# Weight-half splits at the change of block: deferred past the first token block's transposes and put on VectorE

## The chip, the cores and the metric

The kernel runs on one core of one Trainium2 chip. The metric is the device time of one execution in microseconds (us); lower is better. The median of three runs of the kernel before is 1123.03 us (1116.99 to 1123.46).

## The reference

The input is x, 256 tokens by 1024 in float32. It goes through one hybrid layer (attention and an mLSTM side by side, output projection, MLP with a squared ReLU), then through two layers of a second kind, and a last norm. All matrix products that matter here have this shape, with everything else left out:

```python
x = x + rms_norm(mixed @ w_out, g_mix_post)            # "out1"; then the MLP
u = jnp.square(jax.nn.relu(rms_norm(x, g_mlp_pre) @ w_up))
x = x + rms_norm(u @ w_down, g_mlp_post)               # "down"; then layer 0 of the second kind
...
mixed = (g_attn * y_attn + g_conv * y_conv) @ w_out[l]
x = x + (1.0 + gate1) * mixed                          # "out2"; then the feed-forward part
h2 = rms_norm_2(x, norm2_g[l]) * (1.0 + scale2) + shift2
f_gate, f_up = jnp.split(h2 @ w_ffn_in[l], 2, axis=-1)
x = x + (1.0 + gate2) * ((jax.nn.silu(f_gate) * f_up) @ w_ffn_out[l])   # "fo"; then the next layer
```

## The kernel before, in words

**Products.** Each float32 product is made of three matmuls in a rounded float32 type (`mm3`, L281): high by high, high by low, low by high. So every operand is split into a high and a low part. For the weights this is `split` (L193): ScalarE (ACT) casts a loaded half `raw` to `whi` (L199), then GpSimd (POOL, L203) or VectorE (DVE, L205) subtracts and writes `wlo`. Which of the two does it is set by an accumulator: `rot["n"]` grows by `rot["pool"]` (0.75 as a rule) at each split, and POOL takes it when 1 is reached, so three in four go to POOL.

**Weight halves.** A half is 128 x 1024 numbers, 512 KB. A planner list (`plan`) holds them in the order of use, with steps for `ada_w` between them. `do_step` (L208) splits the next half and issues the DMA of the half 8 places on (8 `raw` buffers). `pump` (L221) does steps while `made` is under the smaller of `done + 9 - slack` (9 buffers of `whi` and `wlo`) and `rot["cap"]`. Every product that has used up a half calls `done()`, which calls `tick` and so `pump`. All engines work their instructions in program order.

**Change of block.** The 256 tokens are two token blocks, t = 0 and t = 1. Five times a projection ends in `r_tail` (L387), with the last 5 halves ("out1", "out2") or 6 halves ("down", "fo") of its weight, and is followed by a block whose input needs all of it: out1, down, out2 of layer 0, fo of layer 0, out2 of layer 1. A sixth call, at the end of the kernel, has nothing behind it. `r_tail` does all products of t = 0 first, and behind them the first part of `fin(0)`: `post_norm` (L511; out1 and down) or `post_gate` (L525; out2 and fo), that is the residual, its norm, and the scaled row `xn` (L474 on DVE, L475 on ACT). Then come the products of t = 1, half by half, i = 0, 1, and so on. Ahead of i = `CHAIN` (3), `drain_q(chain)` issues `pre_trans(0)` (L486): 8 transposes on TensorE (L494), gains (L500 DVE, L502 ACT), and the split into `hT` (L552 ACT, L553 DVE). Behind the last product follow `fin(1)`'s residual, norm and `xn`.

The next block starts with `a2_block` (L309). It first makes sure that `hold` halves are split (6 behind out1, 8 behind down and fo, 7 behind out2), then does all `hold` halves for t = 0, with `pre_trans(1)` (the call `before(1)`) issued ahead of the last of them, and then t = 1.

**What sets the splits there.** At its start `r_tail` sets `slack` to 0 and pumps, which leaves 4 halves of the next block split (5-half tails) or 3 (6-half tails). Then `rot["cap"] = state["taken"] + cap` with `cap` 6: the `done()` calls of i = 0, 1 (and 2) split 2 (or 3) more, and these stand in the queues of ACT, POOL and DVE ahead of `pre_trans(0)`. The seventh and eighth half are split in `a2_block`, behind `fin(1)`'s `xn`.

Of the kernel before, what the change touches and what calls it, by code (L numbers as in the profile page):

```python
# [21 lines left out]
NL = 2  # L22
FF1 = 4096
FF2 = 2816
# [3 lines left out]
HB, RB, XB = 9, 8, 4  # L28
SLACK = 2
HOLD0, HOLDZ, HOLDF = 8, 8, 7  # L30
CAP = 6
POOL = 0.75
QKV_TAPS, QKV_POOL = 6, 1.0
GATE_TAPS, GATE_POOL = 4, 1.0
# [3 lines left out]
PRE1, PRE2 = 3, 2  # L38
UPC, GAC = (3, 1), (3, 2)
TAIL = 5  # L40
ST = (1, 1, 4, 1)
EARLY, CHAIN, TWO = 1, 3, 0
GATES = 3
LN = (1, 2, 2)
SIG = (1, 2)
# [10 lines left out]
def tile_hybrid_then_diff(ctx: ExitStack, tc: tile.TileContext, I, out: bass.AP):  # L56
# [9 lines left out]
    def acc_tile():  # L66
        return pp.tile([128, 512], FT, name="bank", bufs=8)
# [6 lines left out]
    def st_tile():  # L74
        return sb.tile([128, 8], FT, name="st", bufs=12)
# [88 lines left out]
    at = {}  # L164
# [8 lines left out]

    raws = {}
    halves = {}
    rot = dict(n=0.0, pool=POOL, cap=1 << 30, slack=SLACK, busy=False)
    state = dict(dma=0, step=0, made=0, taken=0, done=0)
    labels = []

# [28 lines left out]
    def do_step():  # L208
        j, h = divmod(state["step"], 2)
        tag, v, kind = plan[j]  # L210
        r = raws.pop((j, h))
        if kind == "a":
            ada_step(tag, r, h)
        else:
            halves[state["made"]] = split(r, (r.shape[1], r.shape[2]))
            labels.append(tag)
            state["made"] += 1
        state["step"] += 1
        issue_dma()

    def pump(most=99):  # L221
        while state["step"] < 2 * len(plan) and most > 0:
            most -= 1
            if plan[state["step"] // 2][2] != "a" and (
                    state["made"] >= min(state["done"] + HB - rot["slack"], rot["cap"])):
                break
            do_step()

    def take(tag):
        i = state["taken"]  # L230
        assert i < state["made"] and labels[i] == tag, (i, state, tag, labels[i:i + 2])
        state["taken"] = i + 1
        return halves.pop(i)
# [75 lines left out]
    def a2_block(seq, xT, before, evac, hold):  # L309
        rot["slack"] = 0  # L310
        rot["cap"] = state["taken"] + hold
        while state["made"] < state["taken"] + hold:
            pump(1)
        rot["slack"] = SLACK
        ws = [take(tag) for tag, _, _, _ in seq[:hold]]

        def half(out, t, b, k0, kn, w):
            for kk in range(kn):
                k = k0 + kk
                mm_tok(out[b][:, 0:1024 // kn], xT, k, t, w, kk, slice(0, 1024 // kn), k == 0, k == 7)  # L320

        before(0)
        outs = []
        for t in range(2):
            if t == 1:
                rot["cap"] = 1 << 30
                if hold == len(seq):
                    evac(0, outs[0])
            outs.append([acc_tile(), acc_tile()])
            for q in range(hold):  # L330
                half(outs[t], t, *seq[q][1:], ws[q])
                if t == 0 and q == hold - 1 - EARLY:
# [12 lines left out]
        rot["busy"] = False
# [38 lines left out]
                mm_tok(acc[t][n], xT, k, t, w, 0, slice(n * 512, n * 512 + 512), start, stop)  # L384
        done()

    def r_tail(tag, srcs, acc, fin, cap, need=None, last=False):  # L387
        rot["slack"] = 0
        pump()
        ws = [take(tag) for _ in srcs]  # L390
        rot["cap"] = state["taken"] + cap
        def mm(t, n, i):
            mm_tok(acc[t][n], srcs[i][0], srcs[i][1], t, ws[i], 0, slice(n * 512, n * 512 + 512),
                   False, i == len(ws) - 1)

        g = fin(0)
        for n in range(2):
            for i in range(len(ws)):
                if need and n == 0:
                    step_gen(fills2)  # L400
                    need(srcs[i][1])
                mm(0, n, i)
            next(g, None)
        chain.append(g)
        rot["busy"] = True
        g = fin(1)
        ahead = range(len(ws) if last else TWO)
        for i in ahead:
            mm(1, 0, i)
        if last:  # L410
            next(g, None)
        for i in range(len(ws)):
            if i == CHAIN:
                drain_q(chain)
            for n in range(1 if i in ahead else 0, 2):
                mm(1, n, i)
            if i == len(ws) - 1:
                if not last:
                    next(g, None)
# [114 lines left out]
    def fin(post, t, acc, grow, gc, bc):  # L534
        st = st_tile()
        made = []

        def xn_of():
            if not made:
                made.append(xn_tile())  # L540
            return made[0]

        yield from post(t, acc, grow, xn_of, st)
        scale_x(t, made[0], st)
        yield
        yield from pre_trans(t, made[0], hT, gc, bc)
# [154 lines left out]
    made = set()  # L701
# [55 lines left out]
    def mod(l, vec, j):  # L757
        assert (l, vec) in made
        return modc[:, l, vec, j:j + 1]
# [54 lines left out]
    def hid_tile():  # L814
        return ab_tile((128, 2, 2, 256), FR)

    def ffn(ng, pre, prefix, up, down_tag, fin, mid=None, last=False):
        hid = {}
        prefix(hid)
        for g in range(pre, LAG):  # L820
            hid[g] = up(g)
        acc = [[acc_tile() for _ in range(2)] for _ in range(2)]
        for g in range(LAG, ng):
            if mid and g == ng - 3:
                mid()
            hid[g] = up(g)
            if g == LAG:
                assert FDEL < 3
                drain_q(fills)
            h = hid.pop(g - LAG)  # L830
            for kk in range(2):
                r_half(down_tag, h, kk, acc, g == LAG and kk == 0, False)
        srcs = [(hid[g], kk) for g in range(ng - LAG, ng) for kk in range(2)]
        r_tail(down_tag, srcs, acc, lambda t: fin(t, acc[t]), CAP, last=last)

    def hid_from_tok(h, full, t):
        ps = ps_tile().rearrange("p (c t) -> p c t", c=4)
# [54 lines left out]
    def before(t):  # L892
        if t == 1:
            run(pre_trans(1, xn[1], hT, lambda j: col0[:, j:j + 1], None))

    def evac(t, acc):
        for a in range(2):
            A.activation(qk[a][:, t, :], acc[a], AF.Copy)

        def gen():  # L900
            for a in range(2):
                rope(qk[a], t, 0)
                yield
# [167 lines left out]
    hT = new_T()  # L1071
    mlp_c = (lambda j: gcol("g_mlp_pre", j), None)
    r_tail("out1", [(mixT, k) for k in range(8 - TAIL, 8)], acc,
           lambda t: fin(post_norm, t, acc[t], gmix, *mlp_c), CAP, need)
    gmlp = row_tile(I["g_mlp_post"])

    def prefix1(hid):
# [33 lines left out]
    def to_layer(l, fin):  # L1111
        gc = lambda j: mod(l, 1, j)
        bc = lambda j: mod(l, 0, j)
        return lambda t, acc: fin(t, acc, gc, bc)

    def end_mlp(t, acc, gc, bc):
# [2 lines left out]
            hT = new_T()  # L1119
        yield from fin(post_norm, t, acc, gmlp, gc, bc)  # L1120

    ffn(FF1 // 256, PRE1, prefix1, up1, "down", to_layer(0, end_mlp))


    for l in range(NL):
# [178 lines left out]
        g1 = gate_tile(l, 2)  # L1304
# [9 lines left out]
        acc = [[acc_tile() for _ in range(2)] for _ in range(2)]  # L1314
        for k in range(8 - TAIL):
# [1 line left out]
        hT = new_T()  # L1317

        r_tail("out2", [(mixT, k) for k in range(8 - TAIL, 8)], acc,
               lambda t: fin(post_gate, t, acc[t], g1, lambda j: mod(l, 4, j), lambda j: mod(l, 3, j)), CAP)  # L1320
        gfin = row_tile(I["final_g_2"], name="vt") if l == NL - 1 else None
        g2 = []

# [40 lines left out]
        def end_all(t, acc):  # L1364
# [6 lines left out]
                nc.sync.dma_start(out[0, t * 128:(t + 1) * 128, n * 512:(n + 1) * 512], u)  # L1371
            yield

        ffn(FF2 // 256, PRE2, prefix2, up2, "fo", end_all if l == NL - 1 else to_layer(l + 1, end_layer),
            lambda: g2.append(gate_tile(l, 5)), l == NL - 1)


# [25 lines left out]
```

## Time and profile before

| what | value |
|---|---|
| median of 3 runs | 1123.03 us (1116.99, 1123.03, 1123.46) |
| profiled execution, its own time | 1118.56 us |
| its span, first to last instruction | 1116.8 us |
| mean granted TensorE clock | 0.979 of full |
| TensorE (PE) busy | 1052.6 us |
| VectorE (DVE), ScalarE (ACT), GpSimd (POOL) busy | 683.3, 559.8, 709.0 us |
| read from memory | 229.63 MB, 207 GB/s over the span |

A span is shorter than the execution's own time by 1.8 us of work around it. A row of a timeline gives the start and duration in us, the engine, the source line, the operation with its tiles, how many were merged into the row, and in square brackets how long the engine had been idle before it and on whom it had waited. Merged rows overlap a little, since operations of one engine are pipelined; a matmul's duration is longer than the distance to the next.

### The profile page before, as it was taken

How to read it: one execution, taken by the hardware profiler on the slowest of the kernel's cores; microseconds unless marked ns; L12 is line 12 of the kernel's file. 1: busy time of each engine (PE TensorE's matmuls, PEld its weight loads, DVE VectorE, ACT ScalarE, POOL GpSimd, SP SyncE). 2: the span in 40 equal slices, each digit the busy share in tenths (PEclk: the TensorE clock that was granted, in tenths of full speed). 3: DMA queues.
4: the chain of work that ended last, by engine and by line, in shares of the span. 5: the costliest groups of instructions: out<-in, count | busy, mean ns of one | idle time of the engine just before them, and what ended most of it. 6: DMA issues, size and time to landing. Idle time of an engine off the chain costs nothing.

```text
span 1116.8 us, 17204 instructions
## 1 busy us (share of the span) xinstructions
PE 1052.6 (94%) x6435; PEld 927.4 (83%) x6435; DVE 683.3 (61%) x1161; ACT 559.8 (50%) x931; POOL 709.0 (63%) x419
## 2 busy tenths in 40 slices
PE   5969989999999899989999998989999899999997
PEld 4756778998897778988798998878889888999995
DVE  2694535999964387835569688645875455642323
ACT  5535556434455546674633333446466555443441
POOL 5753455665686597665566655757958467567671
PEclk9988999999999999999999999999999899999998
DMA  9562244999996375454599989836535366775631
GB/s 317 138 205 94 76 156 146 320 337 311 343 314 202 95 207 171 151 170 152 150 310 314 333 317 340 310 131 191 176 125 165 121 197 203 239 246 188 197 108 38
DMA packets 170191, 231.82 MB, mean 208 GB/s; under 512 B 10983, under 2 KB 110525, under 8 KB 170107
## 3 DMA queue, kind: packets, MB, share of 16 engines
q1 hardware_dynamic: 169979, 230.71, 63.1%
q8 instruction: 50, 0.82, 0.3%
q14 instruction: 34, 0.28, 0.1%
q0 software_dynamic: 128, 0.02, 0.0%
HBM read 229.63 MB, written 1.06 MB: 207 GB/s over the span
## 4 chain that ended last, share of the span: by engine, by line
PE 53%; DVE 15%; POOL 9%; issue 8%; ACT 7%; DMA 6%; SPq 1%; POOLq 0%; DVEq 0%; ACTq 0%
PE bank L282 16%; PE bank L283 16%; PE bank L284 16%; POOL wlo L203 8%; DVE bank L713 3%; ACT whi L199 3%; DMA raw<-in_w_ffn_in_dram 3%; DVE wlo L205 2%; DMA raw<-in_w_down_dram 2%; SPq L426 1%; DVE modc L738 1%; ACT xn L469 1%; PE bank L792 1%; PE bank L791 1%; DMA raw<-in_w_ffn_out_dram 1%
## 5 line engine op out<-in xcount | busy, mean ns | idle before, releaser
L203 POOL TENSOR_TENSOR wlo<-raw,whi 128x1024 fp32r<-128x1024 f32 x262 | 653.6, 2518 | 308.2 <-ACT whi L199 271.5
L199 ACT ACTIVATE whi<-raw 128x1024 fp32r<-128x1024 f32 x332 | 337.2, 1053 | 78.6 <-DMA raw<-in_w_ffn_in_dram 28.4
L282 PE MATMUL bank<-T,whi 128*128 128x256 f32 x1072 | 309.4, 289 | 6.0 <-ACT sc L1347 2.8
L284 PE MATMUL bank<-T,wlo 128*128 128x256 f32 x1072 | 304.6, 284 | 0.0
L283 PE MATMUL bank<-T,whi 128*128 128x256 f32 x1072 | 304.5, 284 | 0.0
L282 PEld LDWEIGHTS bank<-T,whi 128*128 128x128 f32 x1072 | 206.4, 193 | 13.8 <-issue 5.9
L283 PEld LDWEIGHTS bank<-T,whi 128*128 128x128 f32 x1072 | 206.5, 193 | 1.1
L284 PEld LDWEIGHTS bank<-T,wlo 128*128 128x128 f32 x1072 | 206.5, 193 | 0.0
L205 DVE TENSOR_TENSOR wlo<-raw,whi 128x1024 fp32r<-128x1024 f32 x70 | 126.3, 1805 | 91.3 <-ACT whi L199 91.0
L283 PE MATMUL bank<-wlo,T 128*128 128x512 f32 (+1 forms) x432 | 170.3, 394 | 11.4 <-POOL wlo L203 11.4
L282 PE MATMUL bank<-whi,T 128*128 128x512 f32 (+1 forms) x432 | 173.6, 402 | 3.0 <-ACT T L552 1.5
L284 PE MATMUL bank<-whi,T 128*128 128x512 f32 (+1 forms) x432 | 169.4, 392 | 0.0
L713 DVE SCALAR_TENSOR_TENSOR bank<-raw,cact,bank 128x512 f32<-128x512 f32 x168 | 126.8, 755 | 7.1 <-DMA raw<-in_ada_w_dram 1.8
L282 PE MATMUL bank<-whi,AB 128*128 128x512 f32 x304 | 120.7, 397 | 0.0
L284 PE MATMUL bank<-whi,AB 128*128 128x512 f32 x304 | 120.0, 395 | 0.0
L283 PE MATMUL bank<-wlo,AB 128*128 128x512 f32 x304 | 119.9, 394 | 0.0
L283 PEld LDWEIGHTS bank<-wlo,T 128*128 128x128 f32 x432 | 82.9, 192 | 29.7 <-POOL wlo L203 14.2
L1155 DVE SCALAR_TENSOR_TENSOR bank<-cu,cw,bank 128x256 f32<-128x256 f32 x232 | 104.4, 486 | 4.1
L282 PEld LDWEIGHTS bank<-whi,T 128*128 128x128 f32 x432 | 82.8, 192 | 23.2 <-ACT T L552 2.9
L284 PEld LDWEIGHTS bank<-whi,T 128*128 128x128 f32 x432 | 82.7, 191 | 17.5 <-DVE T L553 0.5
L552 ACT ACTIVATE AB<-bank 128x512 fp32r<-128x512 f32 (+1 forms) x49 | 26.0, 538 | 108.3 <-DVE bank L1351 63.7
L284 PEld LDWEIGHTS bank<-whi,AB 128*128 128x128 f32 x304 | 57.2, 188 | 13.4
(264 smaller groups left out, 1164.1 us busy)
## 6 DMA issues: line engine op xcount, KB each, us to landing
raw<-in_w_in_dram SPq DMA_DIRECT2D x96, 512.0 KB, 5.1
raw<-in_ada_w_dram SPq DMA_DIRECT2D x96, 512.0 KB, 7.4
raw<-in_w_ffn_in_dram SPq DMA_DIRECT2D x88, 512.0 KB, 4.7
raw<-in_w_ffn_out_dram SPq DMA_DIRECT2D x44, 512.0 KB, 5.2
raw<-in_w_up_dram SPq DMA_DIRECT2D x32, 512.0 KB, 5.5
raw<-in_w_down_dram SPq DMA_DIRECT2D x32, 512.0 KB, 8.4
raw<-in_w_out_dram SPq DMA_DIRECT2D x24, 512.0 KB, 4.4
raw<-in_w_attn_o_dram SPq DMA_DIRECT2D x8, 512.0 KB, 3.3
```

Source lines behind the costliest of these rows:

```text
L199: A.activation(hi, r, AF.Copy)
L203: G.tensor_sub(lo, r, hi.bitcast(FT))
L205: V.tensor_sub(lo, r, hi.bitcast(FT))
L282: T.matmul(o, lh, rh, start=start, stop=False)
L283: T.matmul(o, lh, rl, start=False, stop=False)
L284: T.matmul(o, ll, rh, start=False, stop=stop)
L426: nc.sync.dma_start(dst, src)
L469: A.activation(halves_of(xn)[n], halves_of(x[t])[n], AF.Square, scale=1.0 / 32, accum_out=st[:, n:n + 1])
L552: A.activation(dst_hi, full, AF.Copy)
L713: V.scalar_tensor_tensor(ada["sum"], r[:, kk, :], cact[:, k:k + 1], ada["sum"], op0=OP.mult, op1=OP.add)
L738: V.scalar_tensor_tensor(c, c, 0.0 if vec in (0, 3) else 1.0, adab[:, layer, vec, :], op0=OP.add, op1=OP.add)
L1155: V.scalar_tensor_tensor(ca[:, j, :] if k == 30 else sums[j], cu[:, j, k:k + 256], cw[:, l * 4 + j, k:k + 1], sums[j], op0=OP.mult, op1=OP ...
```

## The change

Three things change in `r_tail`. While the t = 1 products run, `cap` is held at what has been made, so no half is split ahead of `pre_trans(0)`. Right behind `pre_trans(0)` the cap becomes 7 ahead, the POOL share becomes 0, so that every split goes to VectorE, and `pump()` splits all that the buffers allow; the share is put back in `a2_block`, behind the splits that it makes itself. And the place of `pre_trans(0)` becomes an argument: `NORM_AT` = 4 for out1 and down (before: 3), `GATE_AT` = 3 for out2 and fo (as before).

```diff
-CAP = 6
+CAP = 7
-EARLY, CHAIN, TWO = 1, 3, 0
+EARLY = 1
+NORM_AT, GATE_AT = 4, 3
...
-    rot = dict(n=0.0, pool=POOL, cap=1 << 30, slack=SLACK, busy=False)
+    rot = dict(n=0.0, pool=POOL, cap=1 << 30, slack=SLACK, busy=False, share=POOL)
...
         while state["made"] < state["taken"] + hold:
             pump(1)
         rot["slack"] = SLACK
+        rot["pool"] = rot["share"]
...
-    def r_tail(tag, srcs, acc, fin, cap, need=None, last=False):
+    def r_tail(tag, srcs, acc, fin, at, need=None, last=False):
         rot["slack"] = 0
         pump()
         ws = [take(tag) for _ in srcs]
-        rot["cap"] = state["taken"] + cap
+        rot["cap"] = state["made"]
...
-        ahead = range(len(ws) if last else TWO)
+        ahead = range(len(ws) if last else 0)
...
         for i in range(len(ws)):
-            if i == CHAIN:
+            if i == at:
                 drain_q(chain)
+                rot["cap"] = state["taken"] + CAP
+                rot["share"], rot["pool"] = rot["pool"], 0.0
+                pump()
```

The calls pass NORM_AT (out1, down) or GATE_AT (out2, fo) in the place of CAP.

VectorE at the change of block behind "down", before: `wlo` is the low part of a weight half, `xn` the normed row, `T_3349` the transposed input `hT` of the next block, `x_69` and `x_70` the residual of t = 0 and t = 1.

```order
L474 TENSOR_SCALAR xn<-x_69,st 128x512
L205 TENSOR_TENSOR wlo<-raw,whi 128x1024
L500 TENSOR_SCALAR bank<-bank,modc 128x128 x2
L553 TENSOR_TENSOR T_3349<-bank,T_3349 128x2x128 x2
L500 TENSOR_SCALAR bank<-bank,modc 128x128 x2
L553 TENSOR_TENSOR T_3349<-bank,T_3349 128x2x128 x2
L517 TENSOR_TENSOR sc<-bank,row 128x512 x2
L522 SCALAR_TENSOR_TENSOR x_70<-sc,st,x_70 128x512 x2
L474 TENSOR_SCALAR xn<-x_70,st 128x512
L500 TENSOR_SCALAR bank<-bank,modc 128x128 x2
```

The same place now (line numbers are 5 higher there, and `split`'s 1 higher):

```order
L479 TENSOR_SCALAR xn<-x_69,st 128x512
L505 TENSOR_SCALAR bank<-bank,modc 128x128 x2
L558 TENSOR_TENSOR T_3349<-bank,T_3349 128x2x128 x2
L505 TENSOR_SCALAR bank<-bank,modc 128x128 x2
L558 TENSOR_TENSOR T_3349<-bank,T_3349 128x2x128 x2
L206 TENSOR_TENSOR wlo<-raw,whi 128x1024 x4
L522 TENSOR_TENSOR sc<-bank,row 128x512 x2
L527 SCALAR_TENSOR_TENSOR x_70<-sc,st,x_70 128x512 x2
L479 TENSOR_SCALAR xn<-x_70,st 128x512
L206 TENSOR_TENSOR wlo<-raw,whi 128x1024
L505 TENSOR_SCALAR bank<-bank,modc 128x128 x2
```

The subtraction ahead of the first block's gains is gone; four stand between the first block's `hT` and the second block's residual, and a fifth between the second block's `xn` and its gains. On GpSimd two subtractions of this place are gone.

ScalarE at the change of block behind out2 of layer 0, before (`T_5157` is `hT`):

```order
L475 ACTIVATE xn<-x_69,st 128x512
L199 ACTIVATE whi<-raw 128x1024 x2
L502 ACTIVATE bank<-bank,modc 128x128 x2
L552 ACTIVATE T_5157<-bank 128x2x128 x2
L502 ACTIVATE bank<-bank,modc 128x128 x2
L552 ACTIVATE T_5157<-bank 128x2x128 x2
L469 ACTIVATE xn,st<-x_70 128x512 x2
L475 ACTIVATE xn<-x_70,st 128x512
L199 ACTIVATE whi<-raw 128x1024
```

And now:

```order
L480 ACTIVATE xn<-x_69,st 128x512
L507 ACTIVATE bank<-bank,modc 128x128 x2
L557 ACTIVATE T_5157<-bank 128x2x128 x2
L507 ACTIVATE bank<-bank,modc 128x128 x2
L557 ACTIVATE T_5157<-bank 128x2x128 x2
L199 ACTIVATE whi<-raw 128x1024 x3
L474 ACTIVATE xn,st<-x_70 128x512 x2
L480 ACTIVATE xn<-x_70,st 128x512
```

The two casts ahead of `pre_trans(0)` and the one behind the second `xn` have become three between the two token blocks' chains.

## Rows read from the trace of the kernel before

**Rows 1.** Busy time, the first line of the page's part 1.

```profile
PE 1052.6 (94%) x6435; PEld 927.4 (83%) x6435; DVE 683.3 (61%) x1161; ACT 559.8 (50%) x931; POOL 709.0 (63%) x419
```

**Rows 2.** Waits of TensorE over the whole span: who was waited for, us in total, times, the longest.

```profile
PE bank L283 <- POOL wlo L203: 11.4, 8, 1.9
...
PE bank L494 <- DVE xn L474: 8.4, 5, 4.2
...
PE bank L282 <- ACT sc L1347: 2.8, 1, 2.8
PE bank L282 <- DVE sc L724: 2.0, 1, 2.0
```

**Rows 3.** Timeline of TensorE at the change of block behind out1: the transposes of t = 0 and of t = 1.

```profile
163.67 1.06 PE L494 MATMUL bank<-ident,xn 128*128 128x128 f32 x8 [1.65 <-DVE xn L474]
...
175.22 1.09 PE L494 MATMUL bank<-ident,xn 128*128 128x128 f32 x8 [0.72 <-DVE xn L474]
```

**Rows 4.** Timeline of TensorE behind down: transposes of t = 0, first product of the next block, its seventh half (two rows), first matmul of t = 1.

```profile
352.67 1.09 PE L494 MATMUL bank<-ident,xn 128*128 128x128 f32 x8 [1.41 <-DVE xn L474]
...
358.62 0.50 PE L282 MATMUL bank<-whi,T 128*128 128x512 f32 x1 [0.66 <-ACT T L552]
...
368.04 0.51 PE L282 MATMUL bank<-whi,T 128*128 128x512 f32 x1 [0.97 <-ACT whi L199]
370.47 0.79 PE L283 MATMUL bank<-wlo,T 128*128 128x512 f32 x1 [1.93 <-POOL wlo L203]
...
375.56 0.39 PE L282 MATMUL bank<-whi,T 128*128 128x512 f32 x1
```

**Rows 5.** Timeline behind down: ACT's casts of the deferred halves, POOL's and DVE's subtractions, DVE's residual and `xn` of t = 1, ACT's next cast.

```profile
352.76 2.94 ACT L199 ACTIVATE whi<-raw 128x1024 fp32r<-128x1024 f32 x3
...
353.88 5.72 POOL L203 TENSOR_TENSOR wlo<-raw,whi 128x1024 fp32r<-128x1024 f32 x2 [1.78 <-ACT whi L199]
...
354.78 2.58 DVE L205 TENSOR_TENSOR wlo<-raw,whi 128x1024 fp32r<-128x1024 f32 x1 [2.17 <-ACT whi L199]
...
363.06 1.42 DVE L522 SCALAR_TENSOR_TENSOR x<-sc,st,x 128x512 f32<-128x512 f32 x2 [0.34 <-POOL st L462]
366.32 0.49 DVE L474 TENSOR_SCALAR xn<-x,st 128x512 f32<-128x512 f32 x1 [1.84 <-POOL st L462]
...
366.95 1.04 ACT L199 ACTIVATE whi<-raw 128x1024 fp32r<-128x1024 f32 x1
```

**Rows 6.** DVE's subtraction L205: the page's group of all 70 (sum in us, mean of one in ns), and one behind out1 that started while POOL had nothing to do.

```profile
L205 DVE TENSOR_TENSOR wlo<-raw,whi 128x1024 fp32r<-128x1024 f32 x70 | 126.3, 1805 | 91.3 <-ACT whi L199 91.0
...
164.74 1.23 DVE L205 TENSOR_TENSOR wlo<-raw,whi 128x1024 fp32r<-128x1024 f32 x1 [1.22 <-ACT whi L199]
```

**Rows 7.** Timeline behind out1: DVE's first two steps of the residual of t = 1, and the first ACT operation behind the `pre_trans` that starts at 175.22.

```profile
169.80 1.29 DVE L517 TENSOR_TENSOR sc<-bank,row 128x512 f32<-128x512 f32 x2
171.42 1.41 DVE L522 SCALAR_TENSOR_TENSOR x<-sc,st,x 128x512 f32<-128x512 f32 x2 [0.34 <-POOL st L462]
...
178.95 0.88 ACT L1086 ACTIVATE sc<-bank 128x512 f32<-128x512 f32 x2
```

**Rows 8.** Timeline of TensorE behind out2 of layer 0, fo of layer 0 and out2 of layer 1: transposes of t = 0, of t = 1, and the wait for the low part of the seventh half.

```profile
534.50 1.06 PE L494 MATMUL bank<-ident,xn 128*128 128x128 f32 x8
546.30 1.04 PE L494 MATMUL bank<-ident,xn 128*128 128x128 f32 x8
549.01 0.50 PE L283 MATMUL bank<-wlo,T 128*128 128x512 f32 x1 [1.43 <-POOL wlo L203]
...
733.92 1.03 PE L494 MATMUL bank<-ident,xn 128*128 128x128 f32 x8
...
751.08 0.51 PE L283 MATMUL bank<-wlo,T 128*128 128x512 f32 x1 [1.93 <-POOL wlo L203]
752.36 1.03 PE L494 MATMUL bank<-ident,xn 128*128 128x128 f32 x8
...
914.40 1.06 PE L494 MATMUL bank<-ident,xn 128*128 128x128 f32 x8 [0.42 <-DVE xn L474]
926.30 1.04 PE L494 MATMUL bank<-ident,xn 128*128 128x128 f32 x8
929.34 0.50 PE L283 MATMUL bank<-wlo,T 128*128 128x512 f32 x1 [1.77 <-POOL wlo L203]
```

**Rows 9.** Timeline at the same three places: DVE's first step of the residual of t = 1 (three rows), its `xn` behind the first of them, and ACT's first cast behind the `pre_trans` that starts at 546.30.

```profile
540.26 0.69 DVE L528 TENSOR_TENSOR bank<-bank,row 128x512 f32<-128x512 f32 x1
544.85 0.49 DVE L474 TENSOR_SCALAR xn<-x,st 128x512 f32<-128x512 f32 x1 [1.85 <-POOL st L462]
550.29 1.06 ACT L199 ACTIVATE whi<-raw 128x1024 fp32r<-128x1024 f32 x1
...
742.35 0.69 DVE L528 TENSOR_TENSOR bank<-bank,row 128x512 f32<-128x512 f32 x1
...
920.59 0.69 DVE L528 TENSOR_TENSOR bank<-bank,row 128x512 f32<-128x512 f32 x1
```

**Rows 10.** Table by stretch: from and to, its length, busy time of PE, PEld, DVE, ACT and POOL with instructions, then the granted TensorE clock (1.00 is full), DMA share and GB/s.

```profile
370.50:373.50 3.00, 3.00 (x9) 2.41 (x10) 0.06 (x1) 0.00 (x0) 2.24 (x1) 0.50 0.58 170
612.80:616.00 3.20, 3.20 (x17) 3.20 (x16) 3.02 (x8) 1.06 (x1) 2.01 (x2) 0.50 1.00 324
...
748.00:754.00 6.00, 3.61 (x19) 2.64 (x19) 0.84 (x2) 2.52 (x5) 4.69 (x2) 1.00 0.27 87
```

More of the change, by code (lines that the diff above doesn't have):

```diff
@@ L815, in hid_tile, with ffn @@
         return ab_tile((128, 2, 2, 256), FR)
-    def ffn(ng, pre, prefix, up, down_tag, fin, mid=None, last=False):
+    def ffn(ng, pre, prefix, up, down_tag, fin, at, mid=None, last=False):
         hid = {}
@@ L833, in ffn @@
         srcs = [(hid[g], kk) for g in range(ng - LAG, ng) for kk in range(2)]
-        r_tail(down_tag, srcs, acc, lambda t: fin(t, acc[t]), CAP, last=last)
+        r_tail(down_tag, srcs, acc, lambda t: fin(t, acc[t]), at, last=last)
     def hid_from_tok(h, full, t):
@@ L1073, in tile_hybrid_then_diff @@
     r_tail("out1", [(mixT, k) for k in range(8 - TAIL, 8)], acc,
-           lambda t: fin(post_norm, t, acc[t], gmix, *mlp_c), CAP, need)
+           lambda t: fin(post_norm, t, acc[t], gmix, *mlp_c), NORM_AT, need)
     gmlp = row_tile(I["g_mlp_post"])
@@ L1120, in end_mlp @@
         yield from fin(post_norm, t, acc, gmlp, gc, bc)
-    ffn(FF1 // 256, PRE1, prefix1, up1, "down", to_layer(0, end_mlp))
+    ffn(FF1 // 256, PRE1, prefix1, up1, "down", to_layer(0, end_mlp), NORM_AT)
     for l in range(NL):
@@ L1319, in tile_hybrid_then_diff @@
         r_tail("out2", [(mixT, k) for k in range(8 - TAIL, 8)], acc,
-               lambda t: fin(post_gate, t, acc[t], g1, lambda j: mod(l, 4, j), lambda j: mod(l, 3, j)), CAP)
+               lambda t: fin(post_gate, t, acc[t], g1, lambda j: mod(l, 4, j), lambda j: mod(l, 3, j)), GATE_AT)
         gfin = row_tile(I["final_g_2"], name="vt") if l == NL - 1 else None
@@ L1372, in end_all @@
             yield
-        ffn(FF2 // 256, PRE2, prefix2, up2, "fo", end_all if l == NL - 1 else to_layer(l + 1, end_layer),
+        ffn(FF2 // 256, PRE2, prefix2, up2, "fo", end_all if l == NL - 1 else to_layer(l + 1, end_layer), GATE_AT,
             lambda: g2.append(gate_tile(l, 5)), l == NL - 1)
```

## The prediction

> **What bounds the kernel now.** First the busy times: TensorE is busy 94% of the span, no other engine over 63% [rows 1], so an edit on the other engines counts only where TensorE waits. Next its waits [rows 2]: the largest sum is for the low parts of weight halves on POOL (L203), then a single wait in the first layer that the change doesn't touch, then the transposes for `xn` (L474). Then the timeline at the five changes of block, since what a wait is worth is read in its place. Behind out1 the transposes wait 1.65 and 0.72 us [rows 3]. Behind down there are waits of 1.41, 0.66, 0.97 and 1.93 [rows 4]. Behind the second-kind blocks it is mainly the low part of the seventh half: 1.43, 1.93, 1.77 [rows 8]. Added up with the small ones this is about 14 us, 1.2% of the time: all that the change can win directly.
>
> **What the change moves.** Seven is the height up to which halves are split; 3 or 4 are split already when `r_tail` starts, so 3 are new behind out1 and the two out2, and 4 behind down and fo. There the eighth still comes behind `xn` of t = 1, now on DVE. Each split is one ACT cast and one subtraction. They leave the way of `pre_trans(0)`, and they land between it and `fin(1)`, on the two in-order engines that do `fin(1)`. So the price is a later `xn` for t = 1, for which the second transposes wait, and behind these all of TensorE's work. The splits' DMAs move along on SP's queue, 4 us later or up to 10 earlier; each is for a half eight places on, in a block where TensorE is fed from buffers, so I cost them at nothing; if that cover is gone, a cast starts late and shows a wait for `raw`.
>
> **Unit costs.** Casts follow each other at 0.98 (three in 2.94), and a subtraction starts 1.1 after its cast does [rows 5]. A subtraction took 1.23 while POOL was idle, and 1.805 on the mean of all 70 [rows 6]. One behind down took 2.58 beside a POOL subtraction that had started 0.9 earlier [rows 5]. After the change POOL has no subtraction in this stretch, so I take 1.23, by the nearest row, and keep 1.805 as the upper end; the lower end is nothing, should they hide.
> The Trainium skill (SBUF — State Buffer, "Who interferes with whom") says that a VectorE tensor_tensor with both inputs in SBUF contends with GpSimd's reads, and that issue order decides who blocks. The 2.58 agrees. By that rule 17 + 2 subtractions cost 1.23 each; by the mean row they would cost 10.9 us more in all.
>
> From the start of the transposes to a free ACT takes 3.99 behind the gated blocks (546.30 to 550.29 [rows 8, 9]) and 3.73 behind out1 (175.22 to 178.95 [rows 3, 7]). Three splits then hold DVE until 3.99 + 1.1 + 3 x 1.23 = 8.8 after the transposes, four until 10.0. One half for one token block costs TensorE 1.41: six took 8.45, from 358.62 to 368.04 - 0.97 [rows 4].
>
> **out1.** `pre_trans(0)` is issued one product later (1.36 for six matmuls), which lets TensorE do work in most of the 1.65 wait; the transposes still start at about 163.67, since `xn` sets them. DVE is held until 163.67 + 3.73 + 1.1 + 3.7 = 172.2. Then come L517 (1.3) and L522, at 173.5 instead of 171.42 [rows 7]. So the second transposes move from 175.22 to 177.3: **+2.1**, although TensorE gets there 1.4 earlier and waits 4.2 in place of 0.72.
>
> **down.** Again one product less to wait: transposes at 352.67, the next block's products from 356.3 instead of 358.62 [rows 4], since no subtraction (DVE until 357.3) is ahead of the gains. Seven halves last until about 366. DVE is held until 352.67 + 10.0 = 362.7, L522 starts at 363.95 instead of 363.06, and `xn` with the second transposes comes at 367.75 (L522 + 3.26 + 0.54 [rows 5]). TensorE waits 1.8. The eighth half: cast from 367.85, subtraction until 370.2, another 1 us of wait; its last five matmuls end at 371.4, and the first of t = 1 runs at about 371.7 instead of 375.56 [rows 4]: **-3.9**.
>
> **out2 of layer 0.** DVE is held until 534.50 + 8.8 = 543.3 instead of starting the residual at 540.26: 3.0 later. From there to `xn` takes 4.59, and 0.63 to the transposes [rows 8, 9]: 548.5 instead of 546.30. The 1.43 for the low part of the seventh half goes. The transposes and six matmuls (0.8 + 1.5) end at 550.8 instead of 549.01 + 1.25 = 550.3: **+0.5**.
>
> **fo of layer 0.** Held until 733.92 + 10.0 = 743.9 instead of 742.35 [rows 8, 9]; transposes at 749.1, the low part of the eighth half at 751.4, first matmul of t = 1 at about 753.0 instead of 752.36 + 0.8 + 1.5 = 754.7: **-1.7**.
>
> **out2 of layer 1.** Held until 914.40 + 8.8 = 923.2 instead of 920.59; transposes at 928.4 instead of 926.30, end at 930.7 instead of 929.34 + 1.25 = 930.6 [rows 8, 9]: **+0.1**.
>
> Sum so far: -2.9.
>
> **The clock.** After the 2.0 us wait for L724 in a feed-forward stage [rows 2], as after 0.97 + 1.93 behind down [rows 4], TensorE ran at 0.50 of its clock, that is 1.2 of 2.4 GHz, for the next three us and more; after the 1.93 behind fo it did not, 1.00 from 748 to 754 [rows 8, 10]. A stretch of 3.2 us at half speed [rows 10] holds 1.6 us of lost work. The new single waits of 4.2, 2.2 and 2.1 (out1, both out2) are above the longest that passed, so I charge each 1.6; behind down the fall that is there today comes again (1.5, which the -3.9 has counted as won). That is 4.8 + 1.5 = +6.3.
> The Trainium skill (TensorE: Matmul & The Clock Gate, "HAM oscillation — how this bites in real kernels") says the same against any change that turns several short waits into one long one: each long pause is paid for again by a stretch at the low rate. By that rule the sum is +3.4, without it -2.9.
>
> **Sum.** -2.9 + 6.3 = +3.4. On the profiled execution (1118.56, of which 1116.8 is span) this gives 1122.0; that execution lies 4.5 under the median of the runs shown, on which it gives 1126.4. I take the middle, **1124.2**: no change that a measurement could tell, which takes about 1% (11 us).
>
> **Rivals.**
> - The clock holds. For it: waits of 1.77 and 1.93 passed [rows 8, 10]. Against: the wait of 2.0 was paid for [rows 2, 10], and all four places would have to be spared. 1124.2 - 6.3 = 1118.
> - The splits hide, in the time that ACT and DVE wait for TensorE anyway: `fin(1)` then starts when `pre_trans(0)` ends, and TensorE waits for no late half. Out1: L517 0.7 behind a free ACT, 168.1 instead of 169.80, -1.7. Down: eight halves from 356.3 (11.3) and the transposes (0.8) end at 368.4 instead of 375.56, -7.2; fo in the same way -3.8. The two out2: transposes and half without the wait (2.3), 548.6 instead of 550.3 and 928.6 instead of 930.6, -1.7 and -2.0. Together -16.4: 1104 (1120.8, the middle of the two scales, less 16.4). Against it stands the order of the instructions: on ACT and DVE the splits are queued ahead of `fin(1)`, and both engines work in order.
> - Slow splits (the other side). The subtractions take the mean of 1.805, at the same places, since something else holds them; all 19 are ahead of what TensorE waits for. Price: 19 x 0.575 = 10.9 on top of +3.4, 1135. It decides from a mean of about 1.6, where the sum passes 11 us. For it: that mean [rows 6]. Against: the long one that can be followed had POOL beside it [rows 5].
> - The turn of POOL and DVE shifts: splits at the changes no longer advance the accumulator, so in the feed-forward stages another half goes to DVE. The 2.0 and 2.8 waits there [rows 2], each with 1.6 of clock, could go or two like them come: -8 or +8, 1116 or 1132.
> - The change does not do what it says: excluded by the order of the instructions; only "seven at once" is 3 or 4 here.
>
> **Chances.** Forecast 0.45 (own range 1118 to 1131); clock holds 0.22; hidden splits 0.08; slow splits 0.12; shifted turn 0.13. Against the median, faster by over 1% is under 1111.8 and slower over 1134.3. Hidden splits and a little of the shifted turn make faster 0.10. Slow splits lie around the upper bound; two thirds of them and a little of the shifted turn make slower 0.10. The rest is 0.80. The range leaves out most of the hidden splits and half of the slow ones: 1111 to 1136.
>
> **What would show it.** Right: no L494 wait at t = 0 behind down; t = 1 transposes waiting 4 us behind out1 and about 2 behind both out2, released by `xn` (L479 there); subtractions of 1.2 to 1.3 between the two chains; no wait for a low part of a seventh half; the clock at 0.50 after the new waits. Wrong: `fin(1)` starting right behind `pre_trans(0)`; subtractions near 2 us; a cast waiting for `raw` there; or gains and losses of over 5 us in the feed-forward stages.

## The result, and the profile after

| | before | after |
|---|---|---|
| median of 18 runs each, us | 1120.05 (1116.06 to 1126.47) | 1127.29 (1121.52 to 1132.97) |
| ratio | | 1.0061 [1.0042, 1.0079] |
| profiled execution, us (span) | 1118.56 (1116.8) | 1132.97 (1131.2) |

The changed kernel is slower by 0.6%, some 7 us. The profiled execution of after is the longest of its 18, so its trace is 14.4 us longer than that of before, twice the difference of the medians. Sizes are therefore taken from several traces wherever there are several.

Part 1 of the page of after, busy times [rows 1]:

```profile
PE 1059.5 (94%) x6435; PEld 932.0 (82%) x6435; DVE 696.9 (62%) x1175; ACT 558.2 (49%) x931; POOL 671.7 (59%) x405
```

VectorE has 14 instructions more, GpSimd 14 fewer: the subtractions that changed hands. (Behind down GpSimd gives up four of the five, not two: the two ahead of the gains, and those of the seventh and eighth half.) TensorE's waits in after, over the span [rows 2]:

```profile
PE bank L499 <- DVE xn L479: 14.4, 7, 5.6
...
PE bank L284 <- POOL wlo L204: 7.5, 7, 1.9
PE bank L283 <- DVE sc L729: 7.3, 2, 4.0
...
PE bank L283 <- DVE fold L740: 5.5, 2, 3.3
...
PE bank L284 <- DVE wlo L206: 1.5, 2, 0.8
```

The exchange that the change was to make is there: waits for a low part on POOL are down from 11.4 to 7.5 us, waits for `xn` up from 8.4 to 14.4. (At the five changes they go from 4.2 to 8.7; the rest, with the longest wait of either trace, 4.2 and 5.6, lies at the start of the kernel.) The two rows in between are not of the changes of block: L729 and L740 belong to the sums of `ada_w` (`ada_step`, `fold`, `ada_reduce`), which VectorE works out beside the matrix products. The two waits for L729 lie in the second feed-forward stage and come to 7.3 instead of 2.0; those for L740 lie in the first and come to 5.5 instead of 1.2.

TensorE at the five changes of block in after, transposes of t = 0 and t = 1 [rows 3, 4, 8]; the L284 rows are waits for the eighth half:

```profile
164.94 1.06 PE L499 MATMUL bank<-ident,xn 128*128 128x128 f32 x8 [0.29 <-DVE xn L479]
...
178.13 1.53 PE L499 MATMUL bank<-ident,xn 128*128 128x128 f32 x8 [3.77 <-DVE xn L479]
...
368.13 1.09 PE L499 MATMUL bank<-ident,xn 128*128 128x128 f32 x8
...
382.80 1.09 PE L499 MATMUL bank<-ident,xn 128*128 128x128 f32 x8 [1.24 <-DVE xn L479]
...
385.24 0.50 PE L284 MATMUL bank<-wlo,T 128*128 128x512 f32 x1 [0.76 <-DVE wlo L206]
...
546.51 1.06 PE L499 MATMUL bank<-ident,xn 128*128 128x128 f32 x8
...
560.16 1.09 PE L499 MATMUL bank<-ident,xn 128*128 128x128 f32 x8 [1.69 <-DVE xn L479]
...
764.45 1.10 PE L499 MATMUL bank<-ident,xn 128*128 128x128 f32 x8
...
766.89 0.50 PE L284 MATMUL bank<-wlo,T 128*128 128x512 f32 x1 [0.77 <-DVE wlo L206]
...
942.68 1.09 PE L499 MATMUL bank<-ident,xn 128*128 128x128 f32 x8 [1.67 <-DVE xn L479]
```

The t = 0 transposes wait for next to nothing; behind out1 and both out2 those of t = 1 wait 3.77, 1.69 and 1.67 for `xn`. No wait for a seventh half is left. What VectorE does between the two chains in after, behind out1 (first two rows), down, and out2 of layer 0 [rows 5, 6, 7, 9]:

```profile
169.75 3.50 DVE L206 TENSOR_TENSOR wlo<-raw,whi 128x1024 fp32r<-128x1024 f32 x3 [0.47 <-ACT whi L200]
173.16 1.28 DVE L522 TENSOR_TENSOR sc<-bank,row 128x512 f32<-128x512 f32 x2
...
373.27 4.63 DVE L206 TENSOR_TENSOR wlo<-raw,whi 128x1024 fp32r<-128x1024 f32 x4 [0.47 <-ACT whi L200]
...
551.62 3.49 DVE L206 TENSOR_TENSOR wlo<-raw,whi 128x1024 fp32r<-128x1024 f32 x3 [0.46 <-ACT whi L200]
555.04 0.68 DVE L533 TENSOR_TENSOR bank<-bank,row 128x512 f32<-128x512 f32 x1
```

A subtraction takes 1.16 to 1.17 us there (4.63 / 4, 3.50 / 3), and the residual of t = 1 starts right behind the last.

**Where the time went.** All kernels here issue the same matmuls in the same order, apart from the transposes of `xn`. So the start of each of the 6,339 others can be set against its start in the trace of before, and the differences read by stage (worked out from the traces, us; minus is gained):

| stage | after | e1 | e2 | e3 | e4 | e5 | e6 | e7 | e8 | e9 | e10 | e11 | e12 |
|---|---|---|---|---|---|---|---|---|---|---|---|---|---|
| out1 | +3.2 | +4.1 | 0.0 | +5.4 | 0.0 | 0.0 | 0.0 | 0.0 | 0.0 | +3.2 | +3.2 | +3.2 | 0.0 |
| first feed-forward | **+11.1** | -0.1 | **+6.9** | -2.2 | -0.1 | **+9.2** | -2.2 | -2.6 | **+9.6** | +6.3 | +4.7 | +5.5 | +1.2 |
| down | -4.4 | -3.1 | -1.1 | +1.4 | -4.5 | -2.6 | 0.0 | -4.5 | -4.5 | -3.8 | -4.0 | -3.8 | +0.1 |
| out2, layer 0 | +0.2 | +0.2 | 0.0 | +2.1 | 0.0 | 0.0 | 0.0 | 0.0 | 0.0 | +0.2 | +0.2 | +0.2 | 0.0 |
| second feed-forward | +3.6 | +1.6 | +0.9 | +2.0 | +1.8 | -0.2 | +2.4 | +2.6 | +3.0 | +2.7 | 0.0 | +3.4 | +2.4 |
| fo, layer 0 | -1.9 | -1.9 | +1.2 | +0.2 | -1.9 | 0.0 | +2.4 | -1.9 | -2.0 | -1.9 | -1.9 | -2.0 | +1.3 |
| out2, layer 1 | -0.6 | -0.6 | 0.0 | -1.3 | +1.3 | +1.3 | -0.3 | -0.3 | +1.2 | -0.6 | -0.6 | -0.6 | +1.6 |

The five changes of block together are worth -3.6 us in after. The loss stands in the first feed-forward stage, where the change edits nothing. Of its 11.1 us, 6.8 are longer waits (9.0 in all, against 2.2 in before), and some 3.4 are two stretches of 3.4 us each at half clock, from 277.6 and 356.1. One trace can be off by 2 us there: e6 runs the program of before in that stage and gains 2.2. (In the second one, behind fo and behind out2 of layer 1, one to two and a half us come and go with the order of before too, as e4 and e12 show.)

### The profile page after: what moved, and what is told of

The parts are those of the page before. It is cut to its first block, busy times and chain, and to the rows that moved or that the text cites. A ratio compares the mean times of both kernels' runs of the same rounds, so it can differ in the third digit from the quotient of the medians.

```text
span 1131.2 us, 17194 instructions
## 1 busy us (share of the span) xinstructions
PE 1059.5 (94%) x6435; PEld 932.0 (82%) x6435; DVE 696.9 (62%) x1175; ACT 558.2 (49%) x931; POOL 671.7 (59%) x405
## 4 chain that ended last, share of the span: by engine, by line
PE 47%; DVE 5%; POOL 5%; ACT 4%; issue 3%; DMA 2%; POOLq 0%; DVEq 0%; ACTq 0%
PE bank L283 15%; PE bank L284 15%; PE bank L285 15%; POOL wlo L204 4%; DMA raw<-in_w_ffn_in_dram 2%; DVE wlo L206 1%; ACT whi L200 1%; DVE bank L718 1%; DMA raw<-in_w_ffn_out_dram 1%; PE bank L797 1%; PE bank L796 1%; DVE x L534 0%; ACT bank L1202 0%; DVE bank L533 0%; DVE bank L505 0%
## 5 line engine op out<-in xcount | busy, mean ns | idle before, releaser
L204 POOL TENSOR_TENSOR wlo<-raw,whi 128x1024 fp32r<-128x1024 f32 x248 | 615.5, 2505 | 314.3 <-ACT whi L200 285.0
L284 PE MATMUL bank<-T,whi 128*128 128x256 f32 x1072 | 305.6, 285 | 0.0
L284 PEld LDWEIGHTS bank<-T,whi 128*128 128x128 f32 x1072 | 207.6, 194 | 1.0
L206 DVE TENSOR_TENSOR wlo<-raw,whi 128x1024 fp32r<-128x1024 f32 x84 | 142.2, 1705 | 93.1 <-ACT whi L200 92.9
L284 PE MATMUL bank<-wlo,T 128*128 128x512 f32 (+1 forms) x432 | 170.3, 394 | 6.8 <-POOL wlo L204 5.2
L718 DVE SCALAR_TENSOR_TENSOR bank<-raw,cact,bank 128x512 f32<-128x512 f32 x168 | 126.8, 754 | 7.8 <-DMA raw<-in_ada_w_dram 2.7
L284 PE MATMUL bank<-wlo,AB 128*128 128x512 f32 x304 | 120.9, 398 | 2.3 <-POOL wlo L204 2.3
L284 PEld LDWEIGHTS bank<-wlo,T 128*128 128x128 f32 x432 | 83.3, 193 | 24.6 <-POOL wlo L204 6.8
L284 PEld LDWEIGHTS bank<-wlo,AB 128*128 128x128 f32 x304 | 57.5, 189 | 15.6 <-POOL wlo L204 3.6
```

Source lines behind the costliest of these rows:

```text
L204: G.tensor_sub(lo, r, hi.bitcast(FT))
L206: V.tensor_sub(lo, r, hi.bitcast(FT))
L284: T.matmul(o, lh, rl, start=False, stop=False)
L718: V.scalar_tensor_tensor(ada["sum"], r[:, kk, :], cact[:, k:k + 1], ada["sum"], op0=OP.mult, op1=OP.add)
```

## The experiments

The accumulator `rot["n"]` gives every fourth subtraction to VectorE. In after the splits at the changes go to VectorE without advancing it, so in each stage behind it is another half's turn: in the first feed-forward stage VectorE has halves 39, 43, ..., 67, ..., 79 instead of 40, 44, ..., 68, ..., 80. Theory T says that this shift makes the loss; rival C, that the changes of block make it. Each run was timed in rounds with the kernel before, e1 to e4, e5 to e8 and e9 to e12 on one chip each; across these groups the ratios are compared, not the medians.

**e1: after, with the turn kept.**

```diff
-        rot["n"] += rot["pool"]
-        if rot["n"] >= 1.0:
+        rot["n"] += rot["pool"] or rot["share"]
+        turn = rot["n"] >= 1.0
+        if turn:
             rot["n"] -= 1.0
+        if turn and rot["pool"]:
```

> The changed kernel, but a split that is forced onto VectorE at a change of block still advances the POOL/VectorE accumulator, so that in the feed-forward stages the same halves go to VectorE as before the change; at the changes nothing differs from the changed kernel. Theory T (the loss is the shifted turn in the feed-forward stages): ratio to before 0.998 to 1.003, the fold waits of 3.3 and 2.2 us in the first feed-forward stage back to about 1.2. Rival C (the loss is at the changes: splits between the two token blocks' chains, or transfers that they defer): ratio stays near 1.006.

Measured: 1118.32 against 1120.52, ratio 0.9975 [0.9958, 0.9992]. TensorE's waits of e1 inside the first feed-forward stage, for the same sums as L740 of after:

```profile
PE bank L285 <- DVE fold L742: 1.1, 1, 1.1
```

The same stage of after:

```profile
PE bank L283 <- DVE fold L740: 5.5, 2, 3.3
PE bank L284 <- POOL wlo L204: 2.3, 3, 1.4
```

And of before:

```profile
PE bank L282 <- DVE fold L735: 1.2, 1, 1.2
```

The scheme at the changes is the same in e1 and after; with the turn kept, 5.5 us of waiting becomes 1.1, close to the 1.2 of before, and the loss of 0.6% a gain of 0.25%.

**e2: before, with the turn alone shifted as in after.**

```diff
+    SHIFT = [0, 3, 5, 3, 5, 3]
...
         rot["slack"] = SLACK
+        rot["n"] = (rot["n"] - 0.75 * SHIFT.pop(0)) % 1.0
```

> The kernel before, with the accumulator moved at each of the five changes by as much as the changed kernel leaves out there (0.75 times 3, 5, 3, 5, 3); splits stay where they were. T: ratio 1.005 to 1.010, with the changed kernel's fold waits of about 3.3 and 2.2 us in the first feed-forward stage. C: ratio 1.000.

Measured: 1126.85, ratio 1.0057 [1.0035, 1.0079]. No split is moved at any change, and the loss is that of after; in the trace 6.9 us of it lie in the first feed-forward stage. T stands from both sides, C falls. One sign that T gave is missing: the wait of 3.3 for `fold` is there, that of 2.2 is not.

**e3: after without the rule that the deferred splits go to VectorE.**

```diff
-        rot["pool"] = rot["share"]
...
-                rot["share"], rot["pool"] = rot["pool"], 0.0
```

> The changed kernel without the VectorE rule: the splits at a change are deferred behind the first block's transposes as there, but take their turns between POOL and VectorE as before, so the turns elsewhere are as before. T: ratio 1.000 to 1.004, a little over the kernel with the turn kept, since POOL's 2.4 us subtractions stand ahead of the norm's two POOL operations of the second token block. C: 1.004 to 1.010.

Measured: 1127.76, ratio 1.0059 [1.0042, 1.0077]: above what T gave, and in C's range. Its first feed-forward stage loses nothing (-2.2); the changes do (+7.8 together), for a reason that after does not have. VectorE in e3 behind down:

```profile
361.57 2.59 DVE L206 TENSOR_TENSOR wlo<-raw,whi 128x1024 fp32r<-128x1024 f32 x1 [1.41 <-ACT whi L200]
...
369.83 1.42 DVE L525 SCALAR_TENSOR_TENSOR x<-sc,st,x 128x512 f32<-128x512 f32 x2 [4.47 <-POOL st L465]
```

And GpSimd there:

```profile
360.67 8.09 POOL L204 TENSOR_TENSOR wlo<-raw,whi 128x1024 fp32r<-128x1024 f32 x3 [5.76 <-ACT whi L200]
368.85 0.30 POOL L464 TENSOR_SCALAR st<-st 128x1 f32<-128x1 f32 x1
```

The norm of t = 1 needs two small steps on GpSimd (L464, L465). Three subtractions stand ahead of them for 8.09 us, and VectorE waits 4.47 for the norm. So deferring alone is a loss, and the VectorE half of the change is worth the 0.8% between e3 and e1.

**e4: the new scheme behind down and fo alone** (tails of six halves); out1 and out2 as before, turn kept.

```diff
...
+        new = len(srcs) == 6
+        rot["cap"] = state["made"] if new else state["taken"] + 6
...
+                if new:
                     rot["cap"] = state["taken"] + CAP
                     rot["share"], rot["pool"] = rot["pool"], 0.0
                     pump()
```

> The changed kernel's scheme only behind the 6-half tails (down and fo of layer 0), the scheme of before behind out1 and both out2, turns kept. T: the two places that gained in the trace stay (together 2 to 5 us), the others as before: ratio 0.995 to 0.999. C: 1.000 to 1.004.

Measured: 1114.36, ratio 0.9944 [0.9929, 0.9959], a little better than T gave, and better than e1 by 3.5 us, about what out1 costs there.

**e5 and e6: before, with the turn shifted by three in the first, or in the second feed-forward stage alone.**

```diff
+    SHIFT = [0, 3, -3, 0, 0, 0]     (e5)
+    SHIFT = [0, 0, 0, 3, -3, 0]     (e6)
...
```

> The kernel before, with the turn of POOL and VectorE moved as in the changed kernel in the first feed-forward stage alone and moved back behind it. T, as the traces place it: most of the 0.6% is here, ratio 1.003 to 1.006, fold waits of over 2 us. If the turn costs the same everywhere it would be 1.002.

> The kernel before, with the same move in the second feed-forward stage (layer 0) alone. T: the rest, ratio 1.000 to 1.002; more than the first stage's part would contradict what the traces place there.

Measured: e5 1126.05, 1.0057 [1.0037, 1.0076]; e6 1120.34, 1.0006 [0.9992, 1.0019]. All that is measured of the loss is in the first stage. In e5's trace 9.2 us are lost there, and 2.6 come back behind down, where the order is that of before.

**e7 and e8: e4 with the turn of the first stage shifted by one, or by two.**

```diff
+    SHIFT = [0, 1, -1, 0, 0, 0]     (e7)
+    SHIFT = [0, 2, -2, 0, 0, 0]     (e8)
...
```

> The kernel that has the new scheme behind down and fo alone (turns kept), with the turn in the first feed-forward stage moved by one split. If the changed kernel's turn is a bad one of four, this one is within 0.3% of the unmoved kernel (ratio to before 0.992 to 0.997); if the turn of before is the only good one, 0.998 to 1.002.

> The same with the turn moved by two splits in the first feed-forward stage. The same two readings: 0.992 to 0.997 if the changed kernel's turn is the bad one, 0.998 to 1.002 if the turn of before is the only good one.

Measured: e7 1109.42, 0.9912 [0.9893, 0.9931], the fastest kernel of the study; e8 1119.75, 1.0009 [0.9988, 1.0030]. So neither reading holds for both: e7 came out below its two ranges, e8 where "the only good one" put it. The number of subtractions that VectorE gets in the stage is nearly the same (15 and 16), yet the two are 1% apart. What differs in the traces is how long they take. A table by stretch counts VectorE's subtractions alone, over the first feed-forward stage (from, to, length, busy time with instructions, clock, DMA share, GB/s). Before:

```profile
180.00:350.00 170.00, 25.05 (x15) 1.00 0.89 306
```

After:

```profile
183.00:363.00 180.00, 35.53 (x15) 0.98 0.82 283
```

e1, with the turn kept:

```profile
182.00:352.00 170.00, 27.17 (x15) 1.00 0.87 300
```

e7 and e8, the least and the largest of these sums:

```profile
177.00:346.00 169.00, 23.44 (x15) 1.00 0.89 308
```

```profile
178.00:357.00 179.00, 42.56 (x16) 0.98 0.84 283
```

Fifteen subtractions of the same size hold VectorE 25 us or 35. Where the time goes is seen best at one of them, VectorE in after (the first three rows are the place of the wait of 3.3 for L740):

```profile
269.61 1.62 DVE L206 TENSOR_TENSOR wlo<-raw,whi 128x1024 fp32r<-128x1024 f32 x1 [2.15 <-ACT whi L200]
271.16 0.74 DVE L716 TENSOR_SCALAR bank<-raw,cact 128x512 f32<-128x512 f32 x1
271.94 2.34 DVE L718 SCALAR_TENSOR_TENSOR bank<-raw,cact,bank 128x512 f32<-128x512 f32 x3
...
305.06 6.39 DVE L206 TENSOR_TENSOR wlo<-raw,whi 128x1024 fp32r<-128x1024 f32 x1
311.37 0.70 DVE L729 STREAM_TRANSPOSE sc<-bank 128x512 f32<-128x512 f32 x1
```

GpSimd in after beside the long one:

```profile
303.21 7.14 POOL L204 TENSOR_TENSOR wlo<-raw,whi 128x1024 fp32r<-128x1024 f32 x3
```

And TensorE in after, in the same stage:

```profile
276.37 0.36 PE L283 MATMUL bank<-T,whi 128*128 128x256 f32 x1 [3.34 <-DVE fold L740]
...
316.06 0.36 PE L283 MATMUL bank<-T,whi 128*128 128x256 f32 x1 [2.20 <-DVE fold L740]
```

The subtraction of half 79 (305.06) started while GpSimd worked through three of its own and took 6.39 us; with the sums of `ada_w` queued behind it, VectorE was late for L740, and TensorE waited 2.20. That of half 67 (269.61) stood 2.15 us at the head of VectorE's queue, waiting for its cast, with L716 and L718 behind it. In before, those sums ran ahead of a subtraction, at 263.54:

```profile
261.14 2.34 DVE L713 SCALAR_TENSOR_TENSOR bank<-raw,cact,bank 128x512 f32<-128x512 f32 x3
263.54 3.06 DVE L205 TENSOR_TENSOR wlo<-raw,whi 128x1024 fp32r<-128x1024 f32 x1
```

The turn alone does not fix these times. e2 has the turn of after, yet its subtraction of half 79 was held for less, and no wait of 2.2 followed:

```profile
299.49 4.04 DVE L206 TENSOR_TENSOR wlo<-raw,whi 128x1024 fp32r<-128x1024 f32 x1
```

**e9 to e12: is it single subtractions (theory L), or the sequence of turns as a whole (rival M)?** Two neighbours exchange engines; the accumulator goes on as it was.

```diff
+    SWAP = {67: True, 68: False}       (e9: after; True is POOL)
+    SWAP = {79: True, 80: False}       (e10: after)
+    SWAP = {67: True, 68: False, 79: True, 80: False}    (e11: after)
+    SWAP = {67: False, 68: True}       (e12: before)
...
+        if SWAP.get(state["made"], turn):
             G.tensor_sub(lo, r, hi.bitcast(FT))
```

> The kernel after, with the engines of weight halves 67 and 68 exchanged in the first feed-forward stage (67 to POOL, 68 to VectorE, as the kernel before has them); the accumulator goes on as in the kernel after. Theory L (single subtractions do the harm: that of half 67 waits 2.15 us for its cast at the head of VectorE's queue, with the gate columns behind it): the wait of 3.3 us for fold goes and the clock behind it, 4.6 us in the matmul-by-matmul difference, so the ratio to before falls from 1.006 to about 1.002. Rival M (the load of the stage as a whole: whichever halves VectorE takes, it is late by the end): the wait moves to another place and the ratio stays above 1.0045.

> The kernel after, with the engines of halves 79 and 80 exchanged in the first feed-forward stage (79 to POOL, 80 to VectorE). Theory L (the subtraction of half 79 is held 6.4 us beside POOL's and makes the gate columns late): the wait of 2.2 us for fold goes, 2.6 us in the difference, ratio about 1.0035; the wait of 3.3 us stays. Rival M: ratio above 1.005, the 2.2 us come elsewhere in the stage.

> The kernel after with both exchanges, 67 with 68 and 79 with 80. Theory L: both waits for fold go, 7.3 us, ratio 0.998 to 1.001, close to the kernel after whose accumulator runs on (0.9975); what is left in the stage is the waits of 0.7 and 1.4 us for low parts on POOL, with 3.7 us at most. Rival M: ratio above 1.0035.

> The kernel before with one exchange and nothing else: half 67 to VectorE, half 68 to POOL. Theory L: a wait of about 3.3 us for fold appears in the first feed-forward stage with the clock behind it, 4.6 us in the difference at most (the kernel before waits 1.2 there already, so 3 to 4.6), ratio 1.003 to 1.004, from one subtraction given to the other engine. Rival M: one exchange is too small to matter, ratio 0.999 to 1.001.

Measured: e9 1126.80, 1.0062 [1.0039, 1.0085]; e10 1124.19, 1.0043 [1.0026, 1.0060]; e11 1124.29, 1.0026 [1.0008, 1.0044]; e12 1122.56, 1.0013 [0.9994, 1.0032]. TensorE's largest waits in the stage, e9:

```profile
PE bank L743 <- DVE AB L562: 2.8, 1, 2.8
PE bank L287 <- DVE fold L744: 2.7, 1, 2.7
```

e10:

```profile
PE bank L287 <- DVE fold L744: 3.3, 1, 3.3
PE bank L743 <- DVE AB L562: 1.2, 1, 1.2
```

e12:

```profile
PE bank L286 <- DVE fold L739: 2.1, 1, 2.1
```

For half 79 the trace of e10 goes with L: the wait of 2.2 is gone, the 3.3 is unchanged. But the ratio cannot decide, since L's 1.0035 and M's 1.005 both lie in its interval (against after it gives 2.0 us; this trace, one of the shortest of e10's runs, 6.4), and in e2 and e9 the wait of 2.2 is missing without this exchange. For half 67, L does not hold: in e9 the first wait only falls from 3.3 to 2.7, that of L743 (L739 in after) grows from 1.2 to 2.8, and the ratio stays. The same exchange the other way round, in e12, brings a wait of 2.1 instead of 1.2 and no measurable loss. e11, with both exchanges, lies between what L and M gave. VectorE is late in the stage by more than these subtractions: in after, e9, e10 and e11 alike, three of the stage's earlier ones took 2.83, 3.21 and 3.20 us, their neighbours in before 2.17, 2.27 and 1.60. So the account is nearer to M, the sum over the sequence. The time of VectorE's subtractions and the time that they wait for their casts at the head of its queue (25.05 + 7.4 in before, 35.53 + 9.3 in after) part the traces in two: sums of 32 to 35 us (before, e1, e3, e4, e6, e7, e12) go with -2.6 to +1.2 us in the stage, sums of 39 to 50 (after, e2, e5, e8 to e11) with +4.7 to +11.1. That the time held on VectorE makes TensorE late is argued from this and from the rows above; no run changed that time and left the order alone.

What stays open: why this turn meets GpSimd's subtractions and another doesn't. It may hang on when DMAs and casts come, and no run held these fixed. Nor is it shown that e7's turn is better than that of before as such: its stage gains 2.6 us, and traces with the turn of before in that stage reach 2.2 (e3, e6).

## Why the prediction was right, and where not

The forecast of 1124.2, no change that can be told, lies 3.1 us under the measured median, and the loss of 0.6% is inside the 1%. (With 18 runs each it could be told all the same; the forecast held that this takes about 1%.) That the number came so near is luck in part: two terms failed, and partly offset each other.

**The sum at the changes (-2.9) was about right.** Measured: -3.6 in after, -2.9 to -3.1 in e9 to e11, -1.3 in e1's trace and -2.8 by e1's ratio. By place:

| | predicted, without the clock | after | e9 to e11 |
|---|---|---|---|
| out1 | +2.1 | +3.2 | +3.2 |
| down | -3.9 | -4.4 | -3.8 to -4.0 |
| out2, layer 0 | +0.5 | +0.2 | +0.2 |
| fo, layer 0 | -1.7 | -1.9 | -1.9 to -2.0 |
| out2, layer 1 | +0.1 | -0.6 | -0.6 |

The measured columns hold what the clock took, which at out1 in after is some 1 us; the predicted column does not. The steps behind the sum hold too. Predicted, VectorE is held until 8.8 us after the transposes of t = 0 behind out2; 546.51 to 551.62 + 3.49 is 8.6. The unit cost of 1.23 for a subtraction came out at 1.17, with no subtraction of GpSimd beside it, so the rival "slow splits" falls; e3 shows one of 2.59 where GpSimd takes part. "The splits hide" falls too, since the residual of t = 1 starts only behind the last of them. The waits came a little under the predicted: 3.77, 1.24, 1.69 and 1.67 for 4.2, 1.8, 2.2 and 2.1.

**The clock (+6.3) failed.** The step was to charge 1.6 for each single wait above 1.93. A table by stretch of after: behind the wait of 3.77, behind the wait of 3.3 for L740, and behind down and both out2 (clock in the column ahead of the last two):

```profile
178.10:181.60 3.50, 3.47 (x14) 2.99 (x15) 2.10 (x6) 2.30 (x8) 0.00 (x0) 0.58 0.16 63
...
276.30:280.00 3.70, 3.63 (x22) 3.66 (x23) 3.60 (x5) 2.26 (x3) 3.48 (x2) 0.68 1.01 339
...
386.20:389.50 3.30, 3.30 (x15) 2.48 (x15) 2.57 (x7) 2.72 (x8) 0.00 (x0) 1.00 0.54 159
...
560.10:563.50 3.40, 3.34 (x19) 2.93 (x20) 2.22 (x7) 2.44 (x7) 0.00 (x0) 1.00 0.00 0
...
942.60:946.00 3.40, 3.32 (x19) 2.92 (x20) 2.22 (x7) 2.45 (x7) 0.00 (x0) 1.00 0.09 35
```

Only out1 paid: +3.2 for +2.1. The two out2 stayed at full clock: their waits came out 0.4 to 0.5 us shorter than worked out, under the longest that had passed in before. The fall behind down did not come back in after. Of 6.3 us about 1 was real here, some 3 in e1's trace by the sizes at out1 and down, where out1 cost +4.1 and down paid again: the rival "the clock holds" (0.22) was the better account of the changes of block. The Trainium skill (TensorE: Matmul & The Clock Gate, "HAM oscillation — how this bites in real kernels") tells of long pauses, in its example waits that outlast the 2 us of work between them; the 3.77 at out1 agrees. That waits near 2 us are paid for too stood in rows of before [rows 2, 10] and not in that section, so "by that rule the sum is +3.4" took it too far, and the two out2 (1.69 and 1.67) are no test of it.

**The turn (a rival at 0.13) decided.** The step that failed is leaving the shifted accumulator out of the sum. The mechanism was written down, with -8 or +8 us, 1116 or 1132, and the mark to look for, losses of over 5 us in the feed-forward stages; e2 and e5 measure it at +0.57%, 6.4 us, and e1 at 0.86% of difference to after. But it was weighed as an accident of either sign. The mean subtraction took 1805 ns where a free one takes 1.23 [rows 6], and the long one that could be followed stood beside GpSimd's [rows 5]: from these rows it could be asked which ones the turn would put there. With 15 or 16 in the first stage they took VectorE from 23 to 43 us (e7, e8). By the ratios, then: -2.8 at the changes with their clock (e1) and +9.6 of turn (from e1 to after) make the +7 that was measured, where the forecast had -2.9 + 6.3. With the order of before at the changes the same turn cost 6.4 (e2, e5); no run shows why it costs more behind the new order.

## What to carry to other kernels

Where one running counter deals work to two engines, an edit at one place re-deals all that follows: keep the counter's turn fixed when only the edited place is to change, and try its few phases by themselves, for here they were worth 1% (e7 against e8), more than the change. Costing the queues around the edited place gave its worth within 2 us; what was missed is a stage that the diff doesn't touch, and setting the traces against each other matmul by matmul finds it at once, though one trace alone can be off by 2 us or more in a stage. A scheme that pays at one kind of place (six-half tails, -0.56%) can lose at another (out1, +3 us): apply it by place.

## What the hardware showed unexpectedly

A VectorE subtraction that started beside a run of three GpSimd subtractions was held 6.39 us (after; 6.38 in e5, 6.39 in e8), longer than two of GpSimd's, against 1.17 with GpSimd idle. The Trainium skill (SBUF — State Buffer, "Who interferes with whom") gives the contention and lets the issue order decide who blocks. On the contention the traces agree. On the order this one does not, by its start times: the VectorE subtraction started at 305.06, ahead of GpSimd's second and third (305.57 and 307.94), and ended behind both. So one VectorE instruction can lose to more than one of GpSimd's in a row. It need not: in before, the one at 263.54 stood inside a run of six and was through in 3.06, and the GpSimd subtraction behind it, from 265.47, took 3.38:

```profile
260.74 15.25 POOL L203 TENSOR_TENSOR wlo<-raw,whi 128x1024 fp32r<-128x1024 f32 x6 [8.61 <-ACT whi L199]
```

The clock did not follow the length of a wait alone. Behind down, 1.24 us for `xn` and 0.76 for the eighth half left it at 1.00 in after; in e1, 1.28 and 0.76 at the same place brought it down:

```profile
371.80:375.20 3.40, 2.52 (x11) 1.87 (x12) 1.98 (x3) 2.07 (x5) 0.00 (x0) 0.81 0.02 7
375.20:378.50 3.30, 3.30 (x11) 2.57 (x11) 2.54 (x7) 2.73 (x8) 0.00 (x0) 0.67 0.54 159
```

And the wait of 1.93 behind fo, which had passed in before [rows 8, 10], was paid for at the same place in e12, whose program is that of before there, while in after one of 1.36, at 355.37, was paid for too. e12, then after:

```profile
754.50:757.80 3.30, 2.85 (x8) 2.27 (x9) 0.00 (x0) 0.00 (x0) 2.71 (x2) 0.50 0.53 145
```

```profile
356.10:359.50 3.40, 3.40 (x10) 2.66 (x9) 0.69 (x1) 0.69 (x2) 3.40 (x2) 0.50 0.89 294
```

So one trace of before could not tell which of its waits are paid for.
